# A hybrid decoder step on one core: products of a column pair without another pair's between them, PSUM banks shared out four and four, and unsplit output weights for the samples

## The chip, the cores and the metric

The kernel runs on one core of a Trainium2 chip. The metric is the time of one execution on the device in microseconds; of several runs the median counts. The profile shows one further execution. PE is the matmul engine (TensorE), DVE is VectorE, ACT is ScalarE, POOL is GpSimd, and SP is the engine that issues most DMAs.

## What is computed

One layer of a decoder trunk for 1024 prompt rows (x_prompt) and 8 sample rows (x_sample) that share all weights, everything in float32. D_MODEL is 1024.

```
h    = rmsnorm(x, norm_gain)
proj = h @ w_in                                   # 10256 columns
q, k, v, gla_g, a_lr, u, pool_g, xq, xg, merge = split(proj)
br_gla  = rmsnorm(gated linear attention(q, k, v, a_lr)) * silu(gla_g)
br_pool = (group maps of trailing means of u, minus u) * pool_scale * silu(pool_g)
br_x    = cross_attn(xq, mem_k, mem_v) * silu(xg)
bproj   = einsum('btnw,nwd->btnd', [br_gla, br_pool, br_x], w_branch)
merged  = sum(sigmoid(merge) * bproj, axis=branch)
out     = rmsnorm(x + merged @ w_out, final_gain)
```

The outputs are out for both groups, the memory's keys and values, and the new states of the attention and of the pool.

## The kernel before

**Precision.** A float32 operand is split into a high part that the matmul takes at full rate (`split`: ACT copies and rounds it, L221) and the rest (DVE subtracts, L222). A product is then three matmuls, high × high (L240), high × low (L241) and low × high (L242), in `mm3`. Operand names carry an h or an l at their end for the two parts.

**Stages.** After loading and normalising x, the wide projection h @ w_in runs in 40 pairs of 256 columns (class `Pair`). A pair is computed by seven products j = 0 to 6, in the manner of Strassen and Winograd: `operands` yields seven left operands, made of the four blocks of the pair's weights (a11, a12, s2, s1, s3, s4, a22), and `RIGHT` names the seven right operands (of h, the same for all pairs). Each product has two halves c (258 columns each) of 12 matmuls. `seq` lists all products in order; `emit` runs the n-th. Left operands are prepared three products ahead (`AHEAD`), which splits them on ACT and DVE, and issues the DMA of the weights of the pair after next.

**Inside a pair** (`run_product`) two banks of PSUM, `p.x`, accumulate j = 0, 2, 4 and 6 in turn, and `p.z` j = 3 and 5; `y` takes j = 1. Between those, ACT saves the sum so far: r1 after j = 0, r2 after j = 2, r3 after j = 4 (all in `saved`, L546). DVE adds y + r1 (L594), z + r3 (L611) and z + r2 (L620), and ACT copies x after j = 6 (L630) or applies silu. A matmul into a bank waits until what reads it is done. The results go to DRAM by DMAs on POOL's queue (`finish`). Before the change the product (i+1, 0) of the next pair stands between (i, 4) and (i, 5).

**Mixers.** Behind every half of a product stands one slot (`fill`), in which steps of the mixers run: the memory's projection, cross attention, gated linear attention, pool. Their matmuls go into banks of the tag pz; those of the products into px. There are eight banks, six px and two pz.

**Branch stage** (L1390 to L1415). 24 units, each with eight k and three tiles of columns (384, 384 and 264), all px; the last three units' results (5, 6, 7 of `merged`) are split late, at L1418: mg5, mg6, mg7.

**Output stage** (from L1424). Two halves of 512 columns; in each eight row blocks of 24 matmuls (k = 0 to 7, three each; `mg` k by w_out k) and a block for the samples (tb 8) of 16 matmuls with 32 columns of samples (`mgs`, not split, L1450), eight for the high and eight for the low part of w_out. They go four at a time into the four row groups of one bank. `w_out_unit` loads a 128 × 512 block of w_out and splits it. x is loaded into y tiles, the row block is added, squared and summed; in the second half the final norm follows (`rstd_of`) and the output's DMAs.

**Order.** PE and SP run in the order of the program (`manual_schedule`); the order on ACT, DVE and POOL is a scheduler's.

Of the kernel before, what the change touches and what calls it, by code (L numbers as in the profile page):

```python
# [47 lines left out]
def trunk_kernel(ctx: ExitStack, tc: tile.TileContext,  # L48
# [195 lines left out]
    def rstd_of(ssq, inv_n, parts=P, more=None):  # L244

        n = ssq.shape[-1]
        v = tiny(n, "rv")[:parts]
        r = tiny(n, "rr")[:parts]
        q = tiny(n, "rq")[:parts]
# [8 lines left out]
        nc.vector.tensor_tensor(q, q, v, op=ALU.mult)  # L258
        last["r"] = nc.vector.scalar_tensor_tensor(r, q, 1.5, r, op0=ALU.add, op1=ALU.mult)
        return r  # L260

# [19 lines left out]
    class Pair:  # L281
# [10 lines left out]
        def operands(self):  # L292
            lo, hi = self.raw
            a11, a12, a21, a22 = lo[:, :, :P], hi[:, :, :P], lo[:, :, P:], hi[:, :, P:]

            def of(x, y, op, s=None):
                s = wk.tile([P, 4, P], F32, tag="ws", name="ws", bufs=2) if s is None else s
                nc.vector.tensor_tensor(s, x, y, op=op)
                return s

            def parts(src, name):
                h, l = W2(name + "h"), W2(name + "l")
                split(h, l, src)
# [12 lines left out]
    def cols_of(off):  # L316
        return w_in[:, off:off + 2 * P]
# [22 lines left out]
    def prepare(n):  # L340

        while prep["n"] < min(n + 1, len(seq)):
            i, j = seq[prep["n"]]
            p = pairs[i]
            if j == 0:
                p.gen = p.operands()
            left[i, j] = next(p.gen)

            if (i, j) == (0, 1):
                pairs[1].load(0)  # L350
            if j == 4 and i + 1 < NPAIR:
                pairs[i + 1].load(1)
            elif j == 6 and i + 2 < NPAIR:
                pairs[i + 2].load(0)
            prep["n"] += 1

# [182 lines left out]
    def run_product(n):  # L539
# [9 lines left out]
        def piece(t, h, c):  # L549
            return t[:, h, c * QT:(c + 1) * QT]  # L550
# [57 lines left out]
        elif j == 4:  # L608
            for c in product(p.x, n, False):
                r3 = saved(p.x, c, "r3")  # L610
                nc.vector.tensor_tensor(piece(p.e1, 1, c), p.z[c][:, :QT], r3, op=ALU.add)  # L611
                if c:
                    gate(p.e1, 1)
                    finish(p.e1, 0)
                yield
        elif j == 5:
            p.e2 = E([2, HT], name="c2")
            mixed(1)
            for c in product(p.z, n, False):
                nc.vector.tensor_tensor(piece(p.e2, 0, c), p.z[c][:, :QT], p.r2[c], op=ALU.add)  # L620
                if c:
                    gate(p.e2, 0)
                yield
        else:
            for c in product(p.x, n, False):
                dst = piece(p.e2, 1, c)
                if p.gated:
                    act(dst, p.x[c][:, :QT], AF.Silu)
                else:
                    nc.scalar.activation(dst, p.x[c][:, :QT], AF.Copy)  # L630
                if c:
                    finish(p.e2, 1)
                yield

# [592 lines left out]
    def emit(n, ahead=AHEAD):  # L1227
# [84 lines left out]
    emit(3, 1)  # L1312
    next(memory)
    for k in range(2):
        operand("22", k, hB[k + 2])
    emit(4)
    for k in range(2):
        nc.vector.tensor_tensor(hA[k + 2], hA[k + 2], t2[k], op=ALU.subtract)
        operand("t4", k, hA[k + 2])

    def branch_k(n, k):
        hi, lo = E([2, HT], F32R, name=f"bh{n}"), E([2, HT], F32R, name=f"bl{n}")
# [29 lines left out]

    br = []
    for n in range(5, len(seq)):
        for _ in range({7: 2, 5: 1, 4: 1, 3: 1, 2: 1, 1: 1}.get(len(seq) - n, 0)):
            br.append(branch_k(ORDER[0], len(br)))
        if n == len(seq) - 2:
            fetch(0)
        emit(n)
# [30 lines left out]
    for u, (o, n, d) in enumerate(units):  # L1390
# [26 lines left out]
    w_out_unit(7, 0)  # L1417
    for d, s in late:  # L1418
        mg_split(d, s)
    for k in range(NK):  # L1420
        w_out_unit(k, 1)

# [1 line left out]
    exp_ln_table()  # L1424
    fg = RAW("fg").rearrange("p a b -> p (a b)")
    nc.sync.dma_start(out=fg, in_=final_gain.partition_broadcast(P))
    ORDERS = ((0, 1, 8, 2, 3, 4, 5, 6, 7), (0, 1, 2, 3, 8, 4, 5, 6, 7))
    rows_, sums = {}, {}
    for hf, order in enumerate(ORDERS):
        for tb in order:  # L1430
            m = P if tb < 8 else NS
            if hf == 0:
                x = (E([D], name="y") if tb < 8 else RAW("ys").rearrange("p a b -> p (a b)"))[:m]
                nc.sync.dma_start(out=x, in_=x_p[tb * P:(tb + 1) * P] if tb < 8 else x_s)
# [6 lines left out]
                nc.vector.tensor_tensor(yl[:, :512], x[:, :512], fg[:, :512], op=ALU.mult)  # L1441
            n, a = hf, 0
            for b in ends:
                t = PX()
                cs = slice(512 * hf + a, 512 * hf + b)
                if tb == 8:

                    for k0, i in ((0, 0), (0, 1), (4, 0), (4, 1)):
                        for j in range(4):
                            nc.tensor.matmul(t[32 * j:32 * j + 32], lhsT=mgs[:, k0 + j], rhs=wo[k0 + j, hf][i].bitcast(F32),  # L1450
                                             start=k0 + i == 0, stop=k0 + i == 5)
                else:
                    c0 = (tb // 4) * HT + (tb % 4) * P
                    for k in range(NK):
                        wh, wl = (w[:, a:b] for w in wo[k, hf])
                        th, tl = (y[:, c0:c0 + P] for y in mg[k])
                        mm3(t[:, :b - a], th, tl, wh, wl, k == 0, k == NK - 1)
# [57 lines left out]
```

## Time and profile before

| | us |
|---|---|
| three runs | 1456.02, 1461.64, 1459.87 |
| median | 1459.87 |
| the profiled execution | 1459.41 |
| its span, first to last instruction | 1457.7 |
| PE busy (98%) | 1433.1 |
| DVE busy (61%) | 893.5 |
| ACT busy (47%) | 688.8 |
| POOL busy (11%) | 159.9 |
| mean granted clock of TensorE | 0.998 |

Rows of the timeline give the start and the duration of an instruction in us, engine, line, operation, output tile and inputs, shapes, and how many alike follow; in brackets stands for how long the engine had been idle and what released it. PE's matmuls overlap: the step from one start to the next is what one costs. A list of waits sums such brackets by waiting tile and releaser. A window's row gives the stretch, its length, the busy time of PE, of its weight loads, of DVE, ACT and POOL (with counts), the granted clock, the DMA engines' busy share and GB/s.

### The profile page before, as it was taken

What the parts mean: (1) busy time and instruction counts of PE and PEld (TensorE: products, weight loads), DVE (VectorE), ACT (ScalarE), POOL (GpSimd) and SP (SyncE); (2) the same over time, 40 slices, a digit from 0 to 9 for tenths busy, and PEclk for the clock granted to TensorE, in tenths of its full rate; (3) what the DMA queues carried; (4) which work ended last, traced back from release to release, by engine and by line L of the source; (5) the groups of instructions that cost most, each with busy time, mean ns of one, the idle gap of its engine ahead of it and who ended that gap; (6) DMA issues with size and microseconds to landing.
All of it is one profiled execution on the core that took longest, in us unless ns stands there. A gap on an engine that the chain in (4) does not pass through costs nothing.

```text
span 1457.7 us, 28253 instructions
## 1 busy us (share of the span) xinstructions
PE 1433.1 (98%) x10849; PEld 1369.9 (94%) x10849; DVE 893.5 (61%) x2051; ACT 688.8 (47%) x1591; POOL 159.9 (11%) x297
## 2 busy tenths in 40 slices
PE   8999999999999999999999999999999999999998
PEld 6899999999999999999999999999999999999686
DVE  6955656655676766767656778775572524554425
ACT  6644435443566666566654544444472423332212
POOL 3112101111111111111111111110010000000000
PEclk9999999999999999999999999999999999999999
DMA  9446665665454554543544455554684687533502
GB/s 331 134 153 197 201 220 178 214 197 174 156 187 143 165 171 135 170 143 121 187 154 150 155 187 168 158 191 154 214 283 146 230 268 252 200 102 95 203 29 88
DMA packets 179666, 255.25 MB, mean 175 GB/s; under 512 B 20412, under 2 KB 130772, under 8 KB 179524
## 3 DMA queue, kind: packets, MB, share of 16 engines
q1 hardware_dynamic: 157724, 179.67, 39.9%
q0 software_dynamic: 21664, 73.59, 13.3%
q8 instruction: 85, 1.39, 0.4%
q14 instruction: 49, 0.40, 0.1%
q10 hardware_dynamic: 144, 0.20, 0.0%
HBM read 176.27 MB, written 77.59 MB: 174 GB/s over the span
## 4 chain that ended last, share of the span: by engine, by line
PE 87%; DMA 6%; DVE 5%; ACT 1%; issue 1%; SPq 0%; DVEq 0%; POOL 0%; ACTq 0%
PE px L240 25%; PE px L241 24%; PE px L242 24%; PE pz L242 2%; PE pz L240 2%; PE pz L241 2%; DMA qb<-xqs 2%; DMA raw<-in_w_in_dram 1%; DVE kc L752 1%; DMA vc<-in_cache_mem_v_dram 1%; PE pz L938 1%; DMA wor<-in_w_out_dram 1%; PE pz L920 1%; DMA x<-in_x_prompt_dram 1%; PE pz L922 1%
## 5 line engine op out<-in xcount | busy, mean ns | idle before, releaser
L242 PE MATMUL px<-bh,wbl 128*128 128x384 f32 (+1 forms) x576 | 184.1, 320 | 0.0
L241 PE MATMUL px<-bl,wbh 128*128 128x384 f32 (+1 forms) x576 | 184.1, 320 | 0.0
L240 PE MATMUL px<-bh,wbh 128*128 128x384 f32 (+1 forms) x576 | 183.7, 319 | 0.0
L546 ACT ACTIVATE r<-px 128x258 f32<-128x258 f32 x240 | 90.1, 376 | 46.7 <-PE px L242 46.0
L240 PEld LDWEIGHTS px<-bh,wbh 128*128 128x128 f32 x576 | 108.4, 188 | 0.0
L241 PEld LDWEIGHTS px<-bl,wbh 128*128 128x128 f32 x576 | 108.2, 188 | 0.0
L242 PEld LDWEIGHTS px<-bh,wbl 128*128 128x128 f32 x576 | 108.2, 188 | 0.0
L240 PE MATMUL px<-ot,s1h 128*128 128x258 f32 x320 | 93.9, 293 | 0.0
L240 PE MATMUL px<-ot,s3h 128*128 128x258 f32 x320 | 93.4, 292 | 0.0
L240 PE MATMUL px<-o,a12h 128*128 128x258 f32 x320 | 93.3, 291 | 0.0
L240 PE MATMUL px<-o,s4h 128*128 128x258 f32 x320 | 93.0, 291 | 0.2 <-DVE c L611 0.2
L240 PE MATMUL px<-o,a11h 128*128 128x258 f32 x320 | 92.9, 290 | 0.0
L240 PE MATMUL px<-ot,a22h 128*128 128x258 f32 x320 | 92.9, 290 | 0.0
L240 PE MATMUL px<-ot,s2h 128*128 128x258 f32 x320 | 92.3, 288 | 0.0
L241 PE MATMUL px<-o,a11h 128*128 128x258 f32 x320 | 91.0, 284 | 0.3 <-DVE o L222 0.3
L242 PE MATMUL px<-o,a12l 128*128 128x258 f32 x320 | 90.7, 284 | 0.0
L241 PE MATMUL px<-o,a12h 128*128 128x258 f32 x320 | 90.6, 283 | 0.0
L241 PE MATMUL px<-ot,s2h 128*128 128x258 f32 x320 | 90.1, 281 | 0.5 <-DVE ot L222 0.5
L242 PE MATMUL px<-o,a11l 128*128 128x258 f32 x320 | 90.6, 283 | 0.0
L241 PE MATMUL px<-ot,a22h 128*128 128x258 f32 x320 | 90.5, 283 | 0.0
L242 PE MATMUL px<-ot,s3l 128*128 128x258 f32 x320 | 90.4, 283 | 0.0
L242 PE MATMUL px<-ot,s1l 128*128 128x258 f32 x320 | 90.4, 282 | 0.0
(473 smaller groups left out, 4590.0 us busy)
## 6 DMA issues: line engine op xcount, KB each, us to landing
raw<-in_w_in_dram SPq DMA_DIRECT2D x80, 512.0 KB, 3.8
msc<-c POOLq DMA_DIRECT2D x24, 516.0 KB, 4.4
brsc<-c POOLq DMA_DIRECT2D x24, 516.0 KB, 3.9
sig<-msc SPq DMA_DIRECT2D x24, 516.0 KB, 6.0
mix<-mixsc SPq DMA_DIRECT2D x48, 256.0 KB, 4.7
brr<-brsc SPq DMA_DIRECT2D x48, 256.0 KB, 5.5
wbr<-in_w_branch_dram SPq DMA_DIRECT2D x24, 512.0 KB, 5.5
acc<-sig POOLq DMA_DIRECT2D x16, 516.0 KB, 4.9
```

Of the source, the lines that this page charges most:

```text
L240: nc.tensor.matmul(out, lhsT=lh, rhs=rh, start=start, stop=False, skip_group_check=more)
L241: nc.tensor.matmul(out, lhsT=lh, rhs=rl, start=False, stop=False, skip_group_check=more)
L242: nc.tensor.matmul(out, lhsT=ll, rhs=rh, start=False, stop=stop, skip_group_check=more)
L546: nc.scalar.activation(r, acc[c][:, :QT], AF.Copy)
L752: nc.vector.tensor_tensor_reduce(kc[:, a, :], kc[:, a, :], qb[:, bb, :], scale=1.0, scalar=0.0, op0=ALU.mult, op1=ALU.add, accum_out=sc[:, ...
L920: nc.tensor.matmul(t[0:64, 0:P], lhsT=ki[:, 0:64], rhs=qi, start=True, stop=True)
L922: nc.tensor.transpose(t[:, P:2 * P], kt, ident)
L938: nc.tensor.matmul(to, lhsT=kiqi[:, 1, cs], rhs=st, start=False, stop=True)
```

## The change

Six edits go together.

1. **Banks**: px 6 to 4, pz 2 to 4. A branch unit's third tile becomes a pz, and the row blocks of the output stage take px and pz by turns.
2. **Order of products**: a pair's seven products stand in one row, 0, 1, 2, 3, 4, 6, 5, without the next pair's product 0 between them. The operands s4 and a22 change places, so do the first pair's right operands "t4" and "22"; the DMA of the pair after next and the end of the pair's second result go from j = 6 to j = 5.
3. **Slots**: the slot behind the first half of j = 4 moves behind its second half, so two slots stand in a row there (`late`). One preparation of a branch operand is one product later.
4. **Start of the output stage**: the first two row blocks run k = 0 to 4 each, then k = 5 to 7 each (`begun`).
5. **Samples**: `own_weights` loads w_out once more, unsplit, by eight DMAs of 512 KB on SP; a half then has 8 sample matmuls instead of 16, in two visits of four (tb 8 and tb 9).
6. **Final norm** (`rstd_of`): −0.5 is multiplied in off the chain, and for one column two DVE operations become one.

```diff
@@ banks
-        return ps.tile([P, 512], F32, tag="px", name="px", bufs=6)
+        return ps.tile([P, 512], F32, tag="px", name="px", bufs=4)
-        return ps.tile([P, 512], F32, tag="pz", name="pz", bufs=2)
+        return ps.tile([P, 512], F32, tag="pz", name="pz", bufs=4)
@@ rstd_of
+        nc.vector.tensor_scalar(hv, v, -0.5, None, op0=ALU.mult)
         last["rr"] = act(r, r, AF.Exp, scale=-0.5)
-        nc.vector.scalar_tensor_tensor(q, r, -0.5, r, op0=ALU.mult, op1=ALU.mult)
-        nc.vector.tensor_tensor(q, q, v, op=ALU.mult)
+        if n == 1:
+            nc.vector.scalar_tensor_tensor(q, r, hv, r, op0=ALU.mult, op1=ALU.mult)
+        else:
+            nc.vector.tensor_tensor(q, r, r, op=ALU.mult)
+            nc.vector.tensor_tensor(q, q, hv, op=ALU.mult)
@@ operands
+            yield parts(a22, "a22")
             yield parts(of(a12, s2, ALU.subtract, s2), "s4")
-            yield parts(a22, "a22")
@@ order
-        seq += [(i, j) for j in range(1, 5)]
-        if i + 1 < NPAIR:
-            seq.append((i + 1, 0))
-        seq += [(i, 5), (i, 6)]
+        seq += [(i, j) for j in (0, 1, 2, 3, 4, 6, 5) if i + j]
@@ emit
-        for _ in run_product(n):
-            fill()
+        late = seq[n][1] == 4
+        for c, _ in enumerate(run_product(n)):
+            if not late:
+                fill()
+            elif c:
+                fill()
+                fill()
@@ branch units
-        ts = [PX() for _ in CH]
+        ts = [PX(), PX(), PZ()]
@@ output stage
+    def own_weights(i):
+        hf, g = divmod(i, 2)
+        for k in range(4 * g, 4 * g + 4, 2):
+            w = E([2, 512], name="wos")
+            nc.sync.dma_start(out=w, in_=w_out[k * P:(k + 2) * P, 512 * hf:512 * hf + 512].rearrange("(k p) n -> p k n", p=P))
+            own.extend([w[:, 0], w[:, 1]])
+    own_weights(0)
...
-    ORDERS = ((0, 1, 8, 2, 3, 4, 5, 6, 7), (0, 1, 2, 3, 8, 4, 5, 6, 7))
+    ORDERS = ((0, 1, 8, 2, 3, 4, 9, 5, 6, 7), (0, 1, 8, 2, 3, 9, 4, 5, 6, 7))
...
+    begun = [PX() for _ in range(2)]
+    turn = [PZ, PX]
+    for ks in (range(5), range(5, NK)):
+        for tb in range(2):
+            row_block(begun[tb], tb, 0, 0, 512, ks)
...
+            if tb >= 8:
+                if tb == 8:
+                    ts = PZ()
+                for j in range(4):
+                    nc.tensor.matmul(ts[32 * j:32 * j + 32], lhsT=mgs[:, 4 * (tb - 8) + j], rhs=own.pop(0),
+                                     start=tb == 8, stop=tb == 9)
+                if 2 * hf + tb < 11:
+                    own_weights(2 * hf + tb - 7)
+                if tb == 8:
+                    continue
+                tb = 8
...
-                t = PX()
+                t = ts if tb == 8 else begun.pop(0) if begun else turn[tb % 2]()
```

What moves shows in three places. The first is ACT in a pair in which no mixers run (one of the last of the 40), from the split before r3 on; r1 and r3 are the saves, c1 and c2 the pair's two results. Before:

```order
L221 ACTIVATE a22h_13623<-raw_13207 128x512 [waits PE_49,Activation_49]
L546 ACTIVATE r3_13641<-px_13391 128x258 [waits PE_49]
L221 ACTIVATE a12h_13664<-raw_13501 128x512 [waits DMAHW6_49,PE_49,Activation_49]
L546 ACTIVATE r3_13656<-px_13392 128x258 [waits PE_49]
L546 ACTIVATE r1_13682<-px_13668 128x258 [waits PE_49]
L75 ACTIVATE c1_13505<-c1_13505 128x516 [waits DVE_49]
L221 ACTIVATE s2h_13702<-ws_13700 128x512 [waits PE_49,Activation_49]
L546 ACTIVATE r1_13696<-px_13669 128x258 [waits PE_49,Activation_49]
```

The same place in the changed kernel:

```order
L221 ACTIVATE a11h_13673<-raw_13324 128x512 [waits PE_49,Activation_49]
L547 ACTIVATE r3_13689<-px_13513 128x258 [waits PE_49]
L221 ACTIVATE a12h_13712<-raw_13549 128x512 [waits DMAHW6_49,PE_49,Activation_49]
L547 ACTIVATE r3_13704<-px_13514 128x258 [waits PE_49]
L75 ACTIVATE c2_13716<-px_13513 128x258 [waits DMASW3_49,PE_49]
L75 ACTIVATE c1_13553<-c1_13553 128x516 [waits DVE_49]
L221 ACTIVATE s2h_13751<-ws_13749 128x512 [waits PE_49,Activation_49]
L75 ACTIVATE c2_13716<-px_13514 128x258 [waits PE_49]
```

Behind the two saves r3 came the next pair's r1; now the copies of j = 6 (c2) come, out of the very banks that r3 was saved from. The split of a12 stands between the two saves in both.

The second place is PE at the start of the output stage, where the late splits mg5, mg6 and mg7 are first read. Before, in the first row block:

```order
L240 MATMUL px_17465<-woh_17390,mg6h_17405 128x512 [waits Activation_49]
L241 MATMUL px_17465<-wol_17391,mg6h_17405 128x512 [waits DVE_49]
L242 MATMUL px_17465<-woh_17390,mg6l_17406 128x512
L240 MATMUL px_17465<-woh_17396,mg7h_17410 128x512 [waits Activation_49]
L241 MATMUL px_17465<-wol_17397,mg7h_17410 128x512 [waits DVE_49]
L242 MATMUL px_17465<-woh_17396,mg7l_17411 128x512 [waits DVE_49]
L240 MATMUL px_17495<-woh_16878,mg0h_16669 128x512
```

In the changed kernel, from the end of the second row block's first part (15 matmuls) on:

```order
L242 MATMUL px_17515<-woh_17344,mg4l_17134 128x512
L240 MATMUL px_17514<-woh_17432,mg5h_17448 128x512 [waits Activation_49]
L241 MATMUL px_17514<-wol_17433,mg5h_17448 128x512 [waits DVE_49]
L242 MATMUL px_17514<-woh_17432,mg5l_17449 128x512
L240 MATMUL px_17514<-woh_17438,mg6h_17453 128x512 [waits Activation_49]
L241 MATMUL px_17514<-wol_17439,mg6h_17453 128x512 [waits DVE_49]
L242 MATMUL px_17514<-woh_17438,mg6l_17454 128x512
L240 MATMUL px_17514<-woh_17444,mg7h_17458 128x512 [waits Activation_49]
L241 MATMUL px_17514<-wol_17445,mg7h_17458 128x512 [waits DVE_49]
L242 MATMUL px_17514<-woh_17444,mg7l_17459 128x512 [waits DVE_49]
L240 MATMUL px_17515<-woh_17432,mg5h_17448 128x512
```

Here 15 matmuls of the second row block (bank 17515) have come between the first block's (17514) mg4 and mg5, so mg7h is the 37th matmul of the stage instead of the 22nd.

The third place is PE at the samples' first visit in the changed kernel, between two row blocks; wos are the unsplit weights, mgs the samples:

```order
L242 MATMUL px_17515<-woh_17444,mg7l_17459 128x512
L1466 MATMUL pz_17574<-wos_17463,mgs_14896 32x512 [waits DMAHW1_49,Pool_49]
L1466 MATMUL pz_17574<-wos_17463,mgs_14896 32x512 [waits Pool_49]
L1466 MATMUL pz_17574<-wos_17465,mgs_14896 32x512 [waits DMAHW2_49,Pool_49]
L1466 MATMUL pz_17574<-wos_17465,mgs_14896 32x512 [waits Pool_49]
L240 MATMUL pz_17586<-woh_16926,mg0h_16717 128x512
```

Before, 16 rows of this kind stood here, eight on the high and eight on the low parts; now four do, which wait for a DMA of their own, and four more follow later in the half.

More of the change, by code (lines that the diff above doesn't have):

```diff
@@ L248, in rstd_of @@
         r = tiny(n, "rr")[:parts]
-        q = tiny(n, "rq")[:parts]
+        q, hv = tiny(n, "rq")[:parts], tiny(n, "rh")[:parts]
         if more is None:
@@ L352, in prepare @@
                 pairs[i + 1].load(1)
-            elif j == 6 and i + 2 < NPAIR:
+            elif j == 5 and i + 2 < NPAIR:
                 pairs[i + 2].load(0)
@@ L615, in run_product @@
                 yield
-        elif j == 5:
+        elif j == 6:
             p.e2 = E([2, HT], name="c2")
             mixed(1)
[L619 to L624, printed above, removed]
             for c in product(p.x, n, False):
@@ L630, in run_product @@
                     nc.scalar.activation(dst, p.x[c][:, :QT], AF.Copy)
+                yield
+        else:
+            for c in product(p.z, n, False):
+                nc.vector.tensor_tensor(piece(p.e2, 0, c), p.z[c][:, :QT], p.r2[c], op=ALU.add)
                 if c:
+                    gate(p.e2, 0)
                     finish(p.e2, 1)
@@ L1314, in trunk_kernel @@
     for k in range(2):
-        operand("22", k, hB[k + 2])
+        nc.vector.tensor_tensor(hA[k + 2], hA[k + 2], t2[k], op=ALU.subtract)
+        operand("t4", k, hA[k + 2])
     emit(4)
     for k in range(2):
-        nc.vector.tensor_tensor(hA[k + 2], hA[k + 2], t2[k], op=ALU.subtract)
-        operand("t4", k, hA[k + 2])
+        operand("22", k, hB[k + 2])
     def branch_k(n, k):
@@ L1354, in trunk_kernel @@
     for n in range(5, len(seq)):
-        for _ in range({7: 2, 5: 1, 4: 1, 3: 1, 2: 1, 1: 1}.get(len(seq) - n, 0)):
+        for _ in range({6: 2, 5: 1, 4: 1, 3: 1, 2: 1, 1: 1}.get(len(seq) - n, 0)):
             br.append(branch_k(ORDER[0], len(br)))
@@ L1419, in trunk_kernel @@
         mg_split(d, s)
+    own = []
+    def own_weights(i):
[5 more added lines that the diff above has]
+    own_weights(0)
     for k in range(NK):
@@ L1426, in trunk_kernel, with row_block @@
     nc.sync.dma_start(out=fg, in_=final_gain.partition_broadcast(P))
-    ORDERS = ((0, 1, 8, 2, 3, 4, 5, 6, 7), (0, 1, 2, 3, 8, 4, 5, 6, 7))
+    ORDERS = ((0, 1, 8, 2, 3, 4, 9, 5, 6, 7), (0, 1, 8, 2, 3, 9, 4, 5, 6, 7))
     rows_, sums = {}, {}
+    def row_block(t, tb, hf, a, b, ks):
+        c0 = (tb // 4) * HT + (tb % 4) * P
+        for k in ks:
+            wh, wl = (w[:, a:b] for w in wo[k, hf])
+            th, tl = (y[:, c0:c0 + P] for y in mg[k])
+            mm3(t[:, :b - a], th, tl, wh, wl, k == 0, k == NK - 1)
+    begun = [PX() for _ in range(2)]
[3 more added lines that the diff above has]
+            row_block(begun[tb], tb, 0, 0, 512, ks)
     for hf, order in enumerate(ORDERS):
@@ L1443, in trunk_kernel @@
             for b in ends:
-                t = PX()
+                t = ts if tb == 8 else begun.pop(0) if begun else turn[tb % 2]()
                 cs = slice(512 * hf + a, 512 * hf + b)
[L1446 to L1457, printed above, removed]
+                if tb < 8 and (hf or tb > 1):
+                    row_block(t, tb, hf, a, b, range(NK))
                 for j in range(4 if tb == 8 else 1):
```

## The prediction

> **What bounds the kernel now.** I read the head of the page first, then its chain of work, then the list of TensorE's waits.
>
> ```profile
> span 1457.7 us, 28253 instructions
> ...
> PE 1433.1 (98%) x10849; PEld 1369.9 (94%) x10849; DVE 893.5 (61%) x2051; ACT 688.8 (47%) x1591; POOL 159.9 (11%) x297
> ...
> PE 87%; DMA 6%; DVE 5%; ACT 1%; issue 1%; SPq 0%; DVEq 0%; POOL 0%; ACTq 0%
> ```
>
> TensorE is busy for 1433.1 of 1457.7 us, so 24.6 us of the span are idle on it; no other engine passes 61%. The change keeps every product and takes away only a few matmuls. What it can gain is therefore a part of those 24.6 us plus those matmuls, and the list of waits says which part.
>
> ```profile
> PE pz L366 <- POOL sel L181: 4.3, 1, 4.3
> PE px L240 <- ACT mg7h L221: 1.7, 1, 1.7
> PE pz L240 <- ACT xqsh L224: 1.4, 1, 1.4
> PE pz L967 <- ACT on L956: 1.3, 1, 1.3
> ...
> PE pz L778 <- DVE ps L773: 1.2, 1, 1.2
> ...
> PE pz L240 <- DVE pTl L222: 0.9, 1, 0.9
> ...
> PE pz L766 <- DVE mkTl L222: 0.6, 1, 0.6
> ...
> PE pz L512 <- ACT mkv L405: 0.5, 1, 0.5
> ...
> PE px L240 <- DVE c L611: 0.2, 1, 0.2
> ```
>
> Each row gives the waiting tile and line, the releaser, then the sum, the count and the longest wait. No row has a pair's matmul waiting for r1, r2 or r3, and only the last one, 0.2 us, waits for another eviction of a product: the new order of the products, the part of the change that runs through all 40 pairs, removes no wait that counts. The 4.3 us at the start, for a constant, stays too.
>
> **mg7, start of the output stage: −2.8.** The timeline of TensorE around it (start, duration, instruction; wait in brackets):
>
> ```profile
> 1351.29 0.40 PE L240 MATMUL px<-woh,mg0h 128*128 128x512 f32 x1
> ...
> 1355.72 0.39 PE L241 MATMUL px<-wol,mg6h 128*128 128x512 f32 x1
> ...
> 1358.03 0.50 PE L240 MATMUL px<-woh,mg7h 128*128 128x512 f32 x1 [1.68 <-ACT mg7h L221]
> ...
> 1359.29 0.50 PE L242 MATMUL px<-woh,mg7l 128*128 128x512 f32 x1 [0.54 <-DVE mg7l L222]
> 1359.63 0.40 PE L240 MATMUL px<-woh,mg0h 128*128 128x512 f32 x1
> ```
>
> The first two rows are 19 steps apart: 4.43 / 19 = 0.233 us each. From the second to the last are 5 steps in 3.91 us, where 5 × 0.233 = 1.17 would do, so the stall costs 3.91 − 1.17 = 2.74, with the slower first matmul behind each wait; I write 2.8. In the new order 36 matmuls, not 21, stand ahead of mg7h: it is asked for at 1351.29 + 36 × 0.233 = 1359.7, and it was ready at 1358.03; mg7l is asked for two steps on, at 1360.1, and was there at 1359.29. So both waits go, with 0.8 us to spare. Behind them nothing is late: mg5 and mg6 were already on time when asked for 15 matmuls sooner. If ScalarE and VectorE came to these splits over 0.8 us later than now, the term would shrink by the excess.
>
> **Samples in the output stage: −3.0.**
>
> ```profile
> 1365.31 1.06 PE L1450 MATMUL px<-woh,mgs 128*32 128x512 f32 x8
> ...
> 1367.91 1.04 PE L1450 MATMUL px<-wol,mgs 128*32 128x512 f32 x8
> 1368.88 0.50 PE L240 MATMUL px<-woh,mg0h 128*128 128x512 f32 x1
> 1369.22 0.39 PE L241 MATMUL px<-wol,mg0h 128*128 128x512 f32 x1
> ...
> 1424.94 1.93 PE L1450 MATMUL px<-wo,mgs 128*32 128x512 f32 x16
> ...
> 1428.51 0.50 PE L240 MATMUL px<-wo,mg0h 128*128 128x512 f32 x1
> ```
>
> A sample block is four groups of four 32-column matmuls, 1365.31 to 1368.88 = 3.57 us, and 1424.94 to 1428.51 = 3.57 in the second half. The next matmul's step is 0.34 instead of 0.23, 0.11 more: 3.68. The last group of four, with its change back to full width, takes 0.97. After the change two visits of one such group stand in each half: 2 × (0.97 + 0.11) = 2.16. Saved: 1.52 per half, 3.0 in all. [...]
>
> The price of it is eight transfers of 512 KB, 4 MB more of w_out to load, on SP's queue.
>
> ```profile
> y<-in_x_prompt_dram SPq DMA_DIRECT2D x8, 512.0 KB, 8.6
> ...
> 1368.81 0.43 SPq L1426 DMA_DIRECT2D fg<-in_final_gain_dram  x1
> ...
> 1376.00:1378.00 2.00, 2.00 (x10) 1.63 (x9) 1.40 (x3) 1.05 (x3) 0.00 (x0) 1.00 1.04 416
> ```
>
> The last row's last two columns say that DMA stands at its full share, 416 GB/s, just after the final gain (issued at 1368.81) and the rows of x are asked for. SP's queue issues in program order, so the first pair of the new weights, 2 × 512 KB ahead of the second half's w_out, can push what follows back by 1.05 MB / 416 GB/s = 2.5 us, to 1371.3. Then the second pair comes behind the gain and two row blocks of x: five transfers of 512 KB, 2.6 MB, 6.3 us at 416 GB/s, landed at 1377.6. Their visit stands five row blocks and one group behind 1351.3: 1351.3 + 120 × 0.233 + 1.1 = 1380.4. The cover is 2.8 us; I cost the loads at nothing, and keep 0 to 3 us for issues later than this. Behind that visit on TensorE stands everything to the end.
>
> **Four banks for mixers: −2.5.** Three of the waits above are for a bank, not for data: the waiting matmul does not read what the releaser writes, but goes into a bank that the releaser was reading.
>
> ```profile
> 291.82 0.39 PE L240 MATMUL pz<-mkTh,xqsh 128*128 128x256 f32 x1 [0.92 <-DVE pTl L222]
> ...
> 168.31 0.38 PE L766 MATMUL pz<-ident,sc 128*8 128x128 f32 x2 [0.58 <-DVE mkTl L222]
> ...
> 35.11 1.08 PE L512 MATMUL pz<-h,wa 128*32 128x258 f32 x16 [0.52 <-ACT mkv L405]
> ...
> 121.82 0.38 PE L240 MATMUL pz<-mkTh,xqsh 128*128 128x256 f32 x1 [1.39 <-ACT xqsh L224]
> ```
>
> The first three sum to 2.02 us. At mg7 a listed wait of 2.22 cost 2.74, a ratio of 1.24; so 2.02 × 1.24 = 2.5. With four banks the bank asked for is two tiles older, and these go. The fourth row is the other kind: the matmul reads xqsh itself. It stays, as do on and ps: 1.4 + 1.3 + 1.2 = 3.9 us of data chains that banks do not shorten. What could take the gain back: each freed matmul finds its own operand late. Bounds 0 and −2.5; I take −2.5, since none of the three rows' operands is named as late.
>
> **Order of the products: +1.0.** Until now a whole product of the next pair stood between the save of r3 (ScalarE, out of the bank of j=4) and the next accumulation into that bank. Now j=6 follows j=4 directly, so each half has 12 matmuls of the other half, and where mixers run also their slots, as its only cover. Rows from a pair without mixers, in time:
>
> ```profile
> 1051.60 0.28 PE L242 MATMUL px<-ot,s3l 128*128 128x258 f32 x1
> ...
> 1051.92 0.39 ACT L546 ACTIVATE r<-px 128x258 f32<-128x258 f32 x1 [0.86 <-PE px L242]
> ...
> 1053.04 0.28 PE L242 MATMUL px<-ot,s3l 128*128 128x258 f32 x1
> ...
> 1053.28 0.63 ACT L221 ACTIVATE a12h<-raw 128x512 fp32r<-128x512 f32 x1 [0.98 <-PE px L241]
> ...
> 1053.82 0.37 ACT L546 ACTIVATE r<-px 128x258 f32<-128x258 f32 x1
> ```
>
> The last matmuls of the two halves start 1.44 us apart, 0.12 each; 13 steps from the last of a half to the first that reuses its bank are 1.56. The first half's save ends at 1052.31, 0.71 behind its matmul; the second's at 1054.19, 1.15 behind, since a split of a12 (0.63) goes first. Both fit, by 0.85 and 0.41 us. The same split stands between the two saves in the new order. The worst of the 80 saves is:
>
> ```profile
> 445.57 0.28 PE L242 MATMUL px<-ot,s3l 128*128 128x258 f32 x1
> ...
> 448.19 0.37 ACT L546 ACTIVATE r<-px 128x258 f32<-128x258 f32 x1
> ```
>
> It ended 448.56 − 445.57 = 2.99 us behind, 1.43 over the cover. A few others are over it by less; two such worst cases, 2.9, are my upper bound, 0 my lower, and 1.0 lies on the side of the many that fit.
>
> **Two slots of mixers in a row: +0.5.** A half of 1.44 us used to stand between any two slots; behind j=4 it no longer does. No row shows this arrangement. If each of the three data waits above grew by the whole 1.44, that would be +4.3; if two of the three vanish for the longer stretch without a slot ahead of them, −2.6. I take +0.5, on the side of a loss, for the cover that goes is certain and the chain that profits isn't.
>
> **The tail: −0.2.**
>
> ```profile
> 1447.96 0.16 DVE L258 TENSOR_TENSOR rq<-rq,rv 128x1 f32<-128x1 f32 x1
> ```
>
> One such VectorE step, 0.16 us, leaves the last chain: some 0.2 with the gap behind it. The 29 rows more on VectorE lie in an engine that is 61% busy: nothing.
>
> **The sum.** −2.8 − 3.0 − 2.5 + 1.0 + 0.5 − 0.2 = −7.0. The profiled execution's own time is 1459.41 (its span 1457.7 and 1.7 around it), half a microsecond under the median of 1459.87. So 1459.41 − 7.0 = **1452.4**. About 0.5%, 7.3 us, is what a measurement of this kernel tells from no change: 1452.6 below, 1467.2 above. The forecast lies just past the lower edge.
>
> **Rivals.** *More goes than I count.* One wait has a tail of its own:
>
> ```profile
> 122.00:124.00 2.00, 1.72 (x9) 1.51 (x10) 0.55 (x1) 0.00 (x0) 0.26 (x1) 0.68 0.99 228
> 124.00:126.00 2.00, 2.00 (x11) 2.00 (x11) 0.69 (x1) 0.21 (x1) 0.00 (x0) 0.50 0.86 258
> ```
>
> Behind the 1.39 us at 121.8 the granted clock (last but two) is 0.68 and 0.50 for two windows: 0.32 × 2 + 0.50 × 2 = 1.6 us lost. If moved slots end that wait, 1.4 + 1.6 = 3.0 more go, near 1449.4. [...] Chance 0.20.
>
> *The product stage gives nothing.* The three bank waits turn into waits for data and doubled slots cost 1.0 instead of 0.5: 1452.4 + 2.5 + 0.5 = 1455.4. For it: 3.9 us of such chains exist. Against: the operands aren't named. Chance 0.20.
>
> *The new weights land late,* by up to 3 us: 1455.4 as well. Chance 0.05.
>
> *ScalarE becomes the bound from j=4 to j=6 (slower).* It decides at 1.56 us from matmul to end of save; now 1.15. Two more operations of 0.63 ahead of the second save make 2.41, 0.85 too late, in each pair where they fall there. Slower by 0.5% needs 7.3 + 7.0 = 14.3 us more than my forecast, 17 pairs; at 20 of 40, 17.0 us: 1469.4. For it: the save at 448 shows that such a queue occurs. Against: only a few of 80 saves did. Chance 0.05.
>
> **How the numbers follow.** Forecast 0.50, of which 0.30 lies under the edge and 0.20 above. Faster: 0.30 + 0.20 = 0.50. Within 0.5%: 0.20 + 0.20 + 0.05 = 0.45. Slower: 0.05. The range goes from 1448 (the first rival, with half of the slots' −2.6 beside it) to 1458 (the second, 1455.4, with 2.6 of the slots' and r3's upper bounds); the last rival and the far ends of the others, 0.2 at most, are left out.
>
> **What would show it.** Waits for mg7h and mg7l absent; two groups at each of four places of some 1.1 us; rows of pTl, mkTl and mkv gone; a row "a22 waits for r" absent or under 2 us in all; no wait for "wos". Wrong would be: bank rows replaced by rows on xqsh, p or on at the same places, a list of r rows counted in tens, or a clock row under 0.7 at a new place.

## The result and the profile after

| | before | changed |
|---|---|---|
| median | 1460.76 us of 4 runs (1456.02 to 1463.89) | 1472.21 us of 4 runs (1469.52 to 1472.86) |
| span of the profiled execution | 1457.7 | 1471.1 |
| mean granted clock of TensorE | 0.998 | 0.993 |

The changed kernel takes 1.0086 times as long, with a 95% interval of 1.0065 to 1.0108. Its median is 11.4 us higher, where a gain of 7.0 was forecast, and outside the range of 1448 to 1458.

The list of TensorE's waits in the changed kernel, its first six rows and two of the smaller ones (waiting tile and line, releaser, sum, count, longest):

```profile
PE px L240 <- ACT r L547: 7.7, 5, 3.4
PE pz L367 <- POOL sel L181: 4.5, 1, 4.5
PE pz L792 <- DMA vc<-in_cache_mem_v_dram: 2.8, 1, 2.8
PE pz L778 <- DVE ps L773: 2.7, 1, 2.7
PE pz L967 <- ACT on L956: 1.7, 1, 1.7
PE pz L240 <- ACT xqsh L224: 1.4, 1, 1.4
...
PE px L487 <- ACT h L494: 0.8, 2, 0.6
...
PE px L487 <- DVE h L497: 0.7, 3, 0.3
```

What was to go has gone: there is no row of mg7, pTl, mkTl or mkv. What came is larger. TensorE waits 7.7 us, in five places, for the save of r, the row that the prediction put at 1.0 us with an upper bound of 2.9. The waits for vc and ps have grown from 0.7 and 1.2 us to 2.8 and 2.7. New, too, are the two rows for h: the transposes at the start (L487) go through px banks, of which there are now four, and wait for what reads them out.

Compared by place, the first matmul of the branch stage comes at 1098.4 instead of 1079.6 (+18.8 us up to there), and the first of the output stage at 1370.5 instead of 1351.3 (+19.2). From there to the end of the span it is 100.6 us instead of 106.4. So the output stage gained 5.8, and what stands ahead of it, the products above all, lost 19.

A part of the 19 is not a wait but a slower clock behind waits. Windows of 2 us in the changed kernel; the last but two column is the granted clock:

```profile
306.00:308.00 2.00, 1.85 (x6) 0.50 (x6) 0.00 (x0) 0.00 (x0) 0.00 (x0) 0.59 0.15 51
308.00:310.00 2.00, 2.00 (x12) 0.86 (x12) 0.00 (x0) 0.05 (x1) 0.00 (x0) 0.56 0.00 0
...
458.00:460.00 2.00, 2.00 (x11) 2.00 (x10) 2.00 (x10) 1.73 (x5) 0.73 (x1) 0.50 0.00 0
460.00:462.00 2.00, 2.00 (x11) 1.44 (x11) 1.41 (x6) 0.80 (x2) 0.97 (x2) 0.50 0.32 131
```

The first two follow the wait for vc, the other two one for r. Summed over all windows up to 1440 us with a clock under 0.95, (1 − clock) × 2 us, such stretches cost 8.4 us here and 1.6 before: 6.8 of the 19. The listed waits of the product stage (without those of the transposes and of the memory at the start) sum to 18.0 instead of 8.9, another 9.1. Of the rest, some 3 us, the transposes' waits make 1.3 (2.3 instead of 1.0); what is left was not traced further.

**How one of the waits for r comes about.** ScalarE of the changed kernel around 341 us:

```profile
344.28 0.47 ACT L75 ACTIVATE p<-pz,nm 128x256 f32<-128x256 f32 x1 [5.21 <-DVE nm L684]
...
345.19 0.38 ACT L547 ACTIVATE r<-px 128x258 f32<-128x258 f32 x1
```

VectorE at the same time:

```profile
341.51 0.42 DVE L752 CUSTOM_DVE_ANT_0 kc<-kc,qb 128x256 f32<-128x256 f32 x1 [3.85 <-DMA qb<-xqs]
...
343.50 0.68 DVE L684 TENSOR_REDUCE nm<-pz 128x2 f32<-128x512 f32 x1
```

And TensorE:

```profile
341.08 0.28 PE L242 MATMUL px<-ot,s3l 128*128 128x258 f32 x1
...
345.63 0.39 PE L240 MATMUL px<-ot,a22h 128*128 128x258 f32 x1 [2.83 <-ACT r L547]
```

The rows are to be read backwards. TensorE's a22 (j = 6) waits for r3 to leave its bank. r3 was due behind the matmul of 341.08, but ScalarE had the softmax's exp (p) ahead of it in its queue, and that waited 5.21 us for a maximum (nm) of VectorE. VectorE had a step of the samples' attention (kc) ahead of nm, which waited 3.85 us for a load (qb). So a load of the mixers, which r3 has nothing to do with, stops TensorE for 2.83 us, by way of two engines on which what stood behind the waiting step began only after it (nm at 343.50 after kc at 341.51, r at 345.19 after p at 344.28). The other large wait, 3.35 us at 457 us, has no exp in it: there ScalarE had a scaling of the attention's state (s) ahead of r3, and that waited for a load itself.

```profile
455.25 0.51 ACT L1005 ACTIVATE s<-s,as 128x256 f32<-128x256 f32 x1 [2.35 <-DMA s<-in_state_gla_dram]
...
456.98 0.36 ACT L547 ACTIVATE r<-px 128x258 f32<-128x258 f32 x1
```

Of the 80 saves of r3, nine end more than 1.56 us behind their last matmul in the changed kernel, the latest 5.0; before, five did, the latest 2.99.

SP's queue shows how a load comes late. Ahead of the wait for vc, which begins at 303 us, in the changed kernel:

```profile
293.16 0.86 SPq L645 DMA_DIRECT2D xq<-xqsc  x1
299.22 0.37 SPq L293 DMA_DIRECT2D raw<-in_w_in_dram  x1
299.64 11.40 SPq L645 DMA_DIRECT2D vc<-in_cache_mem_v_dram  x8
```

SP was done with the load of xq at 294.0 and issued the weight load (raw) at 299.2, 5.2 us later, all of it a wait for VectorE, which had to be done with the buffer that the load goes into. What the mixers load next, vc, stands behind it. The load of the pair after next now stands one product earlier in the program.

How late loads are shows best at the engine that uses them. VectorE's waits for loads, all rows with a DMA as the releaser, sum to 105 us in the changed kernel and to 51 before. The two largest rows after:

```profile
DVE ws L302 <- DMA raw<-in_w_in_dram: 37.6, 23, 3.4
DVE kc L752 <- DMA qb<-xqs: 23.2, 13, 4.0
```

and their counterparts before:

```profile
DVE kc L752 <- DMA qb<-xqs: 18.3, 10, 3.2
...
DVE ws L298 <- DMA raw<-in_w_in_dram: 10.5, 12, 2.0
```

The time that SP itself stands at the weight loads does not show it: over all releasers that is 531 us in 82 waits, against 576 in 76 before. (The 441 and 346 us that some of the expectations below start from are the sums of two and of three rows of SP's list alone; the other rows, most of them with other VectorE instructions as the releaser, are waits of the same loads, and with them the order turns round.)

### The profile page after: what moved, and what is told of

Same layout as the page of the kernel before. It is cut to its first block, busy times and chain, and to the rows that moved or that the text cites. A ratio compares the mean times of both kernels' runs of the same rounds, so it can differ in the third digit from the quotient of the medians.

```text
span 1471.1 us, 28163 instructions
## 1 busy us (share of the span) xinstructions
PE 1438.2 (98%) x10817; PEld 1373.9 (93%) x10817; DVE 896.7 (61%) x2075; ACT 687.3 (47%) x1591; POOL 158.7 (11%) x297
## 3 DMA queue, kind: packets, MB, share of 16 engines
q8 instruction: 85, 1.39, 0.4%
## 4 chain that ended last, share of the span: by engine, by line
PE 88%; DMA 5%; DVE 4%; ACT 2%; issue 1%; SPq 0%; DVEq 0%; ACTq 0%
PE px L240 22%; PE px L241 22%; PE px L242 22%; PE pz L242 5%; PE pz L240 5%; PE pz L241 5%; DMA raw<-in_w_in_dram 1%; DMA qb<-xqs 1%; PE pz L792 1%; DMA x<-in_x_prompt_dram 1%; PE pz L938 1%; PE pz L920 1%; PE pz L922 1%; DVE ot L222 1%; DMA s<-in_state_gla_dram 0%
## 5 line engine op out<-in xcount | busy, mean ns | idle before, releaser
L241 PE MATMUL px<-bl,wbh 128*128 128x384 f32 x384 | 129.6, 338 | 0.0
L240 PE MATMUL px<-bh,wbh 128*128 128x384 f32 x384 | 129.5, 337 | 0.0
L242 PE MATMUL px<-bh,wbl 128*128 128x384 f32 x384 | 129.3, 337 | 0.0
L240 PE MATMUL px<-ot,s1h 128*128 128x258 f32 x320 | 94.2, 294 | 0.5 <-DVE c L595 0.5
L240 PE MATMUL px<-o,a12h 128*128 128x258 f32 x320 | 93.0, 291 | 0.0
L240 PE MATMUL px<-o,s4h 128*128 128x258 f32 x320 | 92.9, 290 | 0.0
L240 PE MATMUL px<-ot,s3h 128*128 128x258 f32 x320 | 91.7, 287 | 0.0
L242 PE MATMUL px<-ot,s2l 128*128 128x258 f32 x320 | 90.9, 284 | 0.0
L242 PE MATMUL px<-ot,a22l 128*128 128x258 f32 x320 | 90.9, 284 | 0.0
L241 PE MATMUL px<-ot,s1h 128*128 128x258 f32 x320 | 90.6, 283 | 0.0
L241 PE MATMUL px<-o,s4h 128*128 128x258 f32 x320 | 90.6, 283 | 0.0
L241 PE MATMUL px<-ot,s3h 128*128 128x258 f32 x320 | 90.6, 283 | 0.0
```

The source lines that it names most:

```text
L240: nc.tensor.matmul(out, lhsT=lh, rhs=rh, start=start, stop=False, skip_group_check=more)
L241: nc.tensor.matmul(out, lhsT=lh, rhs=rl, start=False, stop=False, skip_group_check=more)
L242: nc.tensor.matmul(out, lhsT=ll, rhs=rh, start=False, stop=stop, skip_group_check=more)
```

## The experiments

Two readings were open. **Cover**: r3 has only one half of a product ahead of the matmul that needs its bank, so whatever holds the saving engine stops TensorE. **Loads** (in the expectations the queue theory): the weight load that moved holds the mixers' loads back, and without that nothing would be late. A third, **slots**, blames the two slots of mixers in a row. Each run's time is compared below with the kernel before on the same chip; SP's waits are those at the weight loads over all releasers, VectorE's those for loads, each from one profiled execution.

| run | us | against its before |
|---|---|---|
| changed kernel | 1472.2 | 1.0086 (1.0065 to 1.0108) |
| x1 weight load as before | 1466.1 | 1.0048 (1.0031 to 1.0064) |
| x2 weight loads deferred | 1463.1 | 1.0030 (1.0012 to 1.0047) |
| x3 single slots | 1475.6 | 1.0116 (1.0090 to 1.0142) |
| x4 output stage alone | 1466.0 | 1.0042 (1.0028 to 1.0057) |
| x5 output stage alone, px banks | 1454.0 | 0.9968 (0.9955 to 0.9981) |
| x6 x5 and a weight load deferred | 1452.8 | 0.9957 (0.9940 to 0.9973) |
| x7 next pair's product between | 1456.0 | 0.9973 (0.9963 to 0.9983) |
| x8 x2 and three slots behind j = 4 | 1460.1 | 1.0018 (1.0004 to 1.0032) |
| x9 six and two banks | 1470.1 | 1.0083 (1.0056 to 1.0110) |
| x10 no sample keys | 1465.2 | 1.0044 (1.0029 to 1.0058) |
| x11 x7 and a weight load deferred | 1454.5 | 0.9975 (0.9961 to 0.9989) |
| x12 r3 on VectorE | 1478.9 | 1.0134 (1.0112 to 1.0157) |

**x1, the weight load back in its place.**

```diff
-            elif j == 5 and i + 2 < NPAIR:
-                pairs[i + 2].load(0)
+            elif j == 0 and 0 < i and i + 1 < NPAIR:
+                pairs[i + 1].load(0)
```

> The changed kernel with one edit: the weight load of the pair after next is issued one product later, where it stood before the change. Queue theory (that load, which waits on SP for the subtraction of s4, holds the mixers' loads behind it): SP's waits for raw buffers fall from 441 us towards the 346 us of before, TensorE's waits for r, vc and ps (13.2 us together) fall under 5 us, and the time to 1454 to 1462. Cover theory (one half of a product is too short for the save of r3, whatever the loads do): r waits stay at 6 to 9 us, 1468 to 1474. Slots theory (two slots in a row bring use too close to load): as the cover theory, with vc and ps staying.

Between the two: 1466.1. SP's waits fell from 531 to 490 us, VectorE's from 105 to 80. The wait for ps is gone and that for vc is 0.5 us, but TensorE still waits 7.9 us for r, in seven places. The load's place had a price, some 5 us (6.1 over its before instead of 11.4), and the waits for r do not hang on it.

**x2, both weight loads behind the release of their buffers.**

```diff
-            if j == 4 and i + 1 < NPAIR:
+            if j == 6 and i + 1 < NPAIR:
                 pairs[i + 1].load(1)
-            elif j == 5 and i + 2 < NPAIR:
-                pairs[i + 2].load(0)
+            elif j == 3 and 0 < i and i + 1 < NPAIR:
+                pairs[i + 1].load(0)
```

> The changed kernel with both weight loads of a pair placed one or more products behind the release of their buffer (part 0 at j = 3 of the pair before, part 1 at j = 6), so that SP hardly waits for them. Queue theory: SP's waits for raw fall under 250 us, r, vc and ps under 3 us together, no half-clock stretch behind them, 1450 to 1456. Cover theory: r waits 6 to 9 us, 1468 to 1474. Slots theory: vc and ps stay, 1464 to 1470.

In none of the three ranges, 1463.1. SP's waits fell to 365 us (not under 250) and VectorE's to 76, and still:

```profile
PE px L240 <- ACT r L547: 7.1, 7, 3.5
```

Most of the r waits remain when the loads come earlier, as the cover theory said; the time fell further than it said.

**x3, one slot behind each half of j = 4.**

```diff
-        late = seq[n][1] == 4
+        late = False
```

> The changed kernel with one slot behind each half of j = 4 again. Slots theory: the waits for vc and ps (5.5 us) and the half-clock stretches behind them go, 1463 to 1467. Queue theory: the loads are as late as they were, the waits move to other places but remain over 8 us in all, 1467 to 1475. Cover theory: the first half of j = 4 gains a slot as cover and the second loses one; r waits 4 to 9 us, 1466 to 1474.

1475.6, with 11.1 us of waits for r in nine places, more of both than the cover theory said. The slots theory falls: vc and ps are still waited for, and the time is not lower. The doubled slots are, if anything, of use (the two intervals overlap): behind the second half's save now stand three slots, not two, before its bank is asked for again; behind the first half's stand two either way.

**x4 and x5, the output stage alone.** The kernel before, with the output stage, the unsplit weights and `rstd_of` of the changed one; x5 differs from x4 by one line:

```diff
-    turn = [PZ, PX]
+    turn = [PX, PX]
```

> The kernel before with the output stage and the final norm of the changed kernel alone. By the sum of the prediction 2.8 + 3.0 + 0.2 = 6.0 us are gained: 1454.8 beside 1460.8. A rival, that the new weights' loads push the second half's back: under 3 us gained.

x4 came out slower than before, 1466.0, by a fault of the experiment. With two pz banks one is held by the samples between their visits, and an even row block then has to wait for the other:

```profile
PE pz L240 <- ACT pz L1490: 8.7, 1, 8.7
```

> As x4, but all row blocks of the output stage in px banks (six), so that no row block waits for the bank that the samples hold between their visits (8.7 us in x4). If the output stage is worth the prediction's 6.0 us by itself: 1453 to 1456. If the new loads cost something that the changed kernel's trace hides: over 1457.

1454.0, 4.5 us under its before (the interval is 2.8 to 6.6), which holds the 6.0 of the sum. So this part of the prediction stands, by itself and within the changed kernel, where the stage was 5.8 us shorter. x5 carries the new final norm too, whose 0.2 us no run tells apart.

**x6, x5 with the weight load of the pair after next two products later, in the old order.**

```diff
-            elif j == 6 and i + 2 < NPAIR:
-                pairs[i + 2].load(0)
+            elif j == 2 and 0 < i and i + 1 < NPAIR:
+                pairs[i + 1].load(0)
```

> As x5, and the weight load of the pair after next placed where its buffer has long been free (j = 2 of the pair before), in the old order of products. Queue theory: SP's waits for raw fall from 346 us by 100 or more, but in the old order a product covers r3, so the time falls by 0 to 3 us against x5. Cover theory: no change against x5, within 1 us.

1452.8, 1.2 under x5, with overlapping intervals. SP's waits fell by only 42 us (574 in x5, 532 here) and VectorE's did not fall (56 and 63), so the run says little on loads. It has the lowest time of all.

**x7, the next pair's product 0 between j = 4 and the last two**, with the six and two banks that this needs; the new operand order, the doubled slots, the load at j = 5 and the output stage stay.

```diff
-        seq += [(i, j) for j in (0, 1, 2, 3, 4, 6, 5) if i + j]
+        seq += [(i, j) for j in range(1, 5)]
+        if i + 1 < NPAIR:
+            seq.append((i + 1, 0))
+        seq += [(i, 6), (i, 5)]
```

> The changed kernel with the next pair's product 0 again between j = 4 and the last two (now 6, 5), which needs six px banks and two pz; s4 last, the doubled slots, and the output stage stay. Cover theory: the waits for r (7.7 us) vanish, and what is left of the loss is the late loads: 1458 to 1466. Queue theory: the loads still wait for s4 and the waits for vc and ps stay over 4 us; r waits stay in part, 1462 to 1470.

1456.0, below the ranges of both theories: with a product between again, nothing of the loss is left, not even what was put down to late loads. Its list of waits has no row for r; it begins:

```profile
PE pz L370 <- POOL sel L181: 4.8, 1, 4.8
PE pz L242 <- DVE xq L225: 1.7, 2, 1.0
```

VectorE's waits for loads are 64 us, against 105 in the changed kernel. So the order also sets how late the loads come, and x7 by itself doesn't part cover from loads; x9 and x11 go on from here.

**x8, x2 with the slot behind the second half of j = 3 moved behind j = 4 too.**

```diff
-        late = seq[n][1] == 4
         for c, _ in enumerate(run_product(n)):
-            if not late:
-                fill()
-            elif c:
-                fill()
+            at = seq[n][1], c
+            for _ in range({(3, 1): 0, (4, 0): 0, (4, 1): 3}.get(at, 1)):
                 fill()
```

> x2 (weight loads deferred, 7.1 us of waits for r) with the slot behind the second half of j = 3 also moved behind j = 4, three slots in a row there. Cover theory: what stands ahead of r3 on ScalarE was issued 1.4 us earlier, r waits fall under 4 us, and chains of mixers that now follow one another directly cost 0 to 4 us: 1458 to 1463. If it is only chance which step of the mixers meets r3, r waits stay between 4 and 9 us at other places, 1460 to 1468.

1460.1, within the range of the cover theory; the interval of its ratio overlaps that of x2. The waits for r fall from 7.1 to 1.7 us, and waits in the mixers' own chains (ps 2.3, on 2.4) come in. The edit does two things, which the run doesn't part: what is ahead of r3 on ScalarE was issued earlier, and one slot more stands between a save and the matmul that needs its bank.

**x9, the banks six and two in the changed kernel**, order and all else as changed.

```diff
-        return ps.tile([P, 512], F32, tag="px", name="px", bufs=4)
+        return ps.tile([P, 512], F32, tag="px", name="px", bufs=6)
```

(pz from 4 to 2 with it; branch units and row blocks in px.)

> The changed kernel with six px and two pz banks again, all else as changed: j = 6 still follows j = 4 directly. Cover theory: not the banks but the order makes the loss, so r waits stay at 6 to 11 us, bank waits of 1 to 3 us come back, 1470 to 1477. If the banks made it: r waits under 3 us, 1456 to 1462.

1470.1, with 7.8 us of waits for r, and pTl back:

```profile
PE px L240 <- ACT r L547: 7.8, 7, 2.4
...
PE pz L240 <- DVE pTl L222: 2.1, 1, 2.1
```

**This is the run that decides.** The banks are not the cause. The kernels of x9 and x7 differ in one place, the order of `seq`: 12.2 us over its before the one, 2.6 under it the other. SP's waits are alike in both (530 and 533 us). VectorE's waits for loads are not (110 and 64), so loads do come later in the order without the product between. But late saves occur in both, and only in one do they stop TensorE. A save in x9:

```profile
341.63 0.28 PE L242 MATMUL px<-ot,s3l 128*128 128x258 f32 x1
...
345.37 0.38 ACT L547 ACTIVATE r<-px 128x258 f32<-128x258 f32 x1
...
345.80 0.39 PE L240 MATMUL px<-ot,a22h 128*128 128x258 f32 x1 [2.44 <-ACT r L547]
```

And one in x7, of a second half, whose bank is asked for again at 887.66:

```profile
883.21 0.28 PE L242 MATMUL px<-ot,s3l 128*128 128x258 f32 x1
...
887.01 0.64 ACT L550 ACTIVATE r<-px 128x258 f32<-128x258 f32 x2
...
887.66 0.28 PE L240 MATMUL px<-ot,a22h 128*128 128x258 f32 x1
```

The one begins 3.74 us behind its last matmul, the other 3.80 (the first of the two in its row). In x9 TensorE stands for 2.44 us; in x7 it asks for the bank 4.45 us behind, and doesn't wait. Of the 80 saves, twelve end over 1.56 us behind in x9, the latest 4.1, and seven in x7, the latest 4.2. Nor is the half clock needed for the loss: in x9's profiled execution the windows under 0.95 cost 1.7 us, as before the change (1.6).

**x10, the samples' cached keys and queries not loaded.** VectorE does as many steps on data that is there, so the samples' part of the cross attention is not computed.

```diff
-                nc.vector.tensor_tensor_reduce(kc[:, a, :], kc[:, a, :], qb[:, bb, :],
+                nc.vector.tensor_tensor_reduce(kc[:, a, :], qb, qb,
```

> The changed kernel with the samples' cached keys and queries not loaded: VectorE does the same number of multiply-and-reduce steps for the samples' attention scores, on other data that is there from the start, so that part of the output is not computed. By the chain read from the trace (late query load, VectorE held, softmax's exp on ScalarE held, r3 behind it) the r wait of 3.0 us at 341 and the wait for ps of 2.8 at 364 go, with some 1.6 us of half clock behind them: 1463 to 1467; the r wait at 453, which hangs on other loads, stays at 2.5 to 4. If r3 is late for another reason, 1469 to 1473.

1465.2, with neither the large r wait at 341 nor the wait for ps, while the other large one stays, at 448 us with 2.7 as the longest:

```profile
PE px L240 <- ACT r L547: 5.7, 5, 2.7
```

So those two waits hang on the samples' loads, as the chain of the three views has it. The edit takes the loads of the keys out of SP's queue as well as those of the queries, so it doesn't show each link by itself.

**x11, x7 with the weight load of the pair after next at j = 2 of the pair before**, as in x6.

> x7 (next pair's product 0 between j = 4 and the rest) with the weight load of the pair after next at j = 2 of the pair before. With the cover there, the loads should matter little: x7's 1456.0 less 0 to 3 us. If late loads have a price of their own: 4 us or more less.

1454.5, within the 0 to 3 us (against their own before, 0.9975 beside x7's 0.9973); its list has no row for r either. SP's waits fell by 48 us, to 485, but VectorE waits 84 us for loads, more than in x2 (76). So where the product stands between, loads that hold VectorE as long as in x2 bring no wait for r; in x2 they come with 7.1 us of them. In the changed order deferring two loads took 166 us off SP's waits and 8.4 off the time (11.4 over its before, then 3.1).

**x12, r3 saved by VectorE.**

```diff
-            nc.scalar.activation(r, acc[c][:, :QT], AF.Copy)
+            if name == "r3":
+                nc.vector.tensor_copy(r, acc[c][:, :QT])
+            else:
+                nc.scalar.activation(r, acc[c][:, :QT], AF.Copy)
```

> The changed kernel with r3 saved by VectorE instead of ScalarE; order, banks, slots and loads as changed. If it is ScalarE's queue that makes r3 late (exp held by VectorE at 341, a scaling held by a load at 453), the waits of TensorE for r fall from 7.7 us to 1 to 4, since VectorE is itself held by the late queries for part of the time, and with the half clock behind them the time falls to 1461 to 1468. If r3 is late because of the order alone, on whichever engine, they stay at 6 us or more and the time at 1469 to 1475.

Outside both ranges: 1478.9, and

```profile
PE px L240 <- DVE r L548: 13.4, 9, 4.5
```

It is not ScalarE's queue in particular. VectorE is held by loads as well, and for longer; here by one of the mixers:

```profile
455.16 0.88 DVE L1009 SCALAR_TENSOR_TENSOR s<-vb,smp,s 128x256 f32<-128x256 f32 x2 [5.81 <-DMA vb<-vs]
...
458.31 0.40 DVE L548 COPY r<-px 128x258 f32<-128x258 f32 x1
```

From the last matmul of j = 4 to the first of j = 6, less one step, the place by 341 did get better (1.5 us instead of 3.0), and the one by 454 worse (4.6 instead of 3.5). Three more, of 1.7 to 2.1 us, come in pairs behind the mixers, from 1035 us on.

## Why the prediction was wrong, point by point

*mg7, samples and tail, −6.0:* right. The stage was 5.8 us shorter, the mg7 rows are gone, and x5 has the gain by itself. The new weights were never waited for.

*Four banks, −2.5:* right for the rows named, which are absent, and come back with two pz banks (x9: pTl 2.1). What it left out is the other side: with four px banks the transposes at the start wait 2.3 us instead of 1.0 (1.0 in x9, with six). In the times the term can't be told: x9, without those banks, came out no slower than the changed kernel.

*Order of the products, "+1.0", bounds 0 and 2.9:* **this is the step that failed.** The mechanism was named, the half of 1.56 us as r3's only cover. The term was 1.0 us; TensorE's waits for r came to 7.7, and the saves ended up to 5.0 us behind. Its size was read off the 80 saves of r3 before, of which the worst was 2.99 us behind. But those rows show what stood ahead of r3 in the old order, and which step of the mixers meets which product changed with the order. A wider bound lay in ScalarE's own list of waits of the kernel before, which the prediction didn't read:

```profile
ACT p L75 <- DVE nm L684: 42.1, 16, 4.7
```

These are sixteen waits of the exp alone, up to 4.7 us, and any of them could come to stand before r3. Against a cover of 1.56 one such is some 3 us. One did (2.83 us at 345 us); the other large wait had a load of the state ahead of it (3.35 at 457). The prediction wrote that the new order "removes no wait that counts", from the absence of r rows. That absence was the work of the product in between, the cover that the change took away: x7, which puts it back, has saves as late as x9's and no wait for r.

*Two slots in a row, +0.5:* no cost shows. x3, without them, came out at 1475.6, with intervals that overlap.

*What was not in the sum at all:* the weight load that moves one product forward on SP, past which the mixers' loads have to wait. The prediction followed the saves on ScalarE, and not what stands behind that load on SP. In this order, putting it back is worth some 5 us (x1), and deferring both weight loads 8.4 (x2); with the product between again, deferring it shows no gain (x7 0.9973, x11 0.9975).

*The rivals:* the one on the slower side, ScalarE's queue as the bound from j = 4 to j = 6, named the right place, with a chance of 0.05 and a price of 0.85 us in each of 20 pairs. What came was up to 3.4 us in five places, and x12 shows that ScalarE is not special in it. That this rival's 1469.4 lies near the measured time is luck. The half clock was weighed as something that might go (1.6 us) and not as something that each new wait of some 3 us might bring: 6.8 us in the profiled execution.

What stays open is how the 14.8 us between x9 and x7 divide. In the two profiled executions, 13.7 us apart, TensorE's listed waits differ by 9.7 us, of which 7.8 are the waits for r; but r is late in part because loads are, and the order makes loads late (VectorE waits 110 us for them in x9, 64 in x7). x2 comes nearest to parting the two: it has the order of x9 and VectorE waits 76 us. It takes 0.57% more than x7 against its before, where x9 takes 1.10% more. By this estimate about half of the difference comes without late loads and half with them; that x2 has four px banks and x7 six is not allowed for.

## What to carry to other kernels

An absent wait can be the work of what stands between two instructions; before that is taken away, read how long the engine behind it can be held by anything at all (here ScalarE, by 5.21 us at p), not how late this instruction was in the old order. Where a load moves in a queue, ask what stands behind it. The old order of products with the new output stage (x5, 0.9968 of before; x6, with a deferred weight load, 0.9957, not told apart from it) is faster than both kernels.

## What the runs showed of the hardware

The half clock behind a wait (windows of 2 us with a granted clock of 0.50 to 0.59) comes in some places and not in others. In the changed kernel the waits of 2.8 us for vc, 2.7 for ps, 3.4 for r and 1.7 for on (at 767 us) had one each, that of 2.83 at 345 us had none; in x9 waits of 2.1 to 2.4 us for pTl, r and ps had none, and one of 2.4 for r at 456 us had; before, one of 1.39 us had it and one of 1.68 not. So in these runs the length of a wait did not tell whether the half clock came behind it: the wait for xqsh that had it before, with 1.39 us at 121.8, had none in the changed kernel, with 1.44 us at 122.3. In x2 the runs of one program went from 1458.6 us, at a mean granted clock of 0.998, to 1470.0 at 0.994.

A matmul on split operands (128 × 258) stepped 0.12 us; one on operands that are not split (128 × 256, L396) 0.22: sixteen of them took the 3.55 us from 46.04 to 49.59 of the kernel before.
